# Rotary key at the front of the layer on 128 partitions, raw latents into their own norm, GLA values scaled by ScalarE

## Chip, cores, metric

The kernel runs on one core of one Trainium2 chip. The metric is the device time in microseconds (us) of one execution. Engines are called as in the profile: PE (TensorE matmuls), PEld (its weight loads), DVE (VectorE), ACT (ScalarE), POOL (GpSimd), SP (the queue that issues most DMAs). Matrix products run in a split form: each operand is written as a high part and a low part in a 32-bit matmul format, and three products (high·high, low·high, high·low) are added up.

## What is computed

Two layers of a hybrid encoder on 1024 tokens of width 1024. Cut to what the change touches:

```python
u = rmsnorm(h, ln_mix[i]) @ w_in[i]
(c_q, c_kv, k_rope, gate_a, gq, gk, gv, lr_f, lr_b, gate_g) = split_cols(u, IN_SPLITS)
# mla_branch
q  = (rmsnorm(c_q, q_norm) @ w_uq)          # q_nope and q_rope of 4 heads
kv = (rmsnorm(c_kv, kv_norm) @ w_ukv)       # k_nope and v of 4 heads
k_r = apply_rope(k_rope, pos)               # [x1*cos - x2*sin, x1*sin + x2*cos], one key for all heads
s = qn @ k_nope^T + qr @ k_r^T ; prob = softmax(s * scale) ; o = prob @ v
# gla_branch: gq, gk, gv with decays, in chunks, forward and backward, then a norm per head
h = h + concat(mla * silu(gate_a), gla * silu(gate_g)) @ w_out[i]
h = h + sigmoid(rmsnorm(h, ple_norm[i]) @ w_ple_gate[i]) * (p[i] @ w_ple_proj[i])
```

The first norm is never applied to x. The kernel multiplies the raw x (with the gain folded in) by w_in, and scales each product afterwards by r_x, the reciprocal root mean square of each token.

## The kernel before, in words

Everything is kept with features on partitions and the 1024 tokens along the free axis. SBUF tiles of 128x1024 come from one pool of 41 buffers (`mt`), PSUM from two tags, "mm" and "aux", with two buffers of 128x1024 each. A matmul tile of the input projection (`in_tile`) is 48 matmuls of 512 columns into one PSUM buffer; the buffer comes free when the last engine that reads it is done. Weights are loaded raw by SP (L141, two buffers), split by ACT into high part (L142) and negated copy (L146), and the low part is finished by an adding DMA on POOL's queue (L147); five pairs of split halves are kept ahead.

Within a layer the order of steps is a string of two-character words (`ORDER`, L50 and L51), one letter for the step and one digit for the head or tile. The framework's planner then orders the instructions of each engine by that priority and by its own modelled times, so neighbouring steps interleave, and each engine runs its queue strictly in that order. The letters that matter here:

- K, Q: the two pairs of GLA keys and queries. `in_qk` L330 to L334: two DVE products with r_x out of PSUM per tile.
- R: `rotary_tables`, first layer only. cos and sin for 1024 positions, computed on 128 partitions as 4 blocks of 256 positions by 32 frequencies, and written to DRAM (`cosd`, `sind`, L274).
- V: `in_v` L337 to L357, GLA values of two heads with tokens on partitions; L354 scales each of two PSUM buffers by `rc`, the column form of r_x, on DVE.
- S, O: GLA state and output of a head. S holds a chain of 28 small DVE steps (L456) and the masked copy L468; O ends in an own norm: ACT copies and squares PSUM (L102, L497), ACT and DVE split the squares (L128, L129), PE adds them over partitions (L181).
- C, D: two and three latent tiles. `latent_tile` L503 to L508: DVE multiplies PSUM by r_x (L506), ACT squares the result (`SquareSum`, L211 or L214), DVE adds the squares up (L215).
- N, M: `latent_norm` L510 to L518, norm of the C or D latents and their split.
- G, A: gates of GLA and MLA. L362 is a DVE product of PSUM with r_x, L363 the Silu on ACT.
- X: `q_pairs` L570, the two rotary query tiles, which stay in the two "aux" PSUM buffers, and cos and sin read back from DRAM (L576).
- E: `rotary_key` L579 to L595. Rows 64 to 127 of `small` (made by `in_small`, L315, ahead of all steps) are rotated: six DVE products of 32x1024 (L584 to L589), two ACT copies (L591, L592) and two DVE differences (L594) of 64x1024. The result `ks`, `kl` is first read by the attention scores (L667).
- H, T: query heads (L597) and `rotary_queries` (L603): per half two DVE products out of the "aux" buffers (L609, L610), a sum (L611), a split, and DMAs into `qs` (L619).
- k, v, s, b: keys, values, scores and outputs of the attention (L625, L633, L656, L693).

`rstd` (L170) makes a reciprocal root: matmul with ones, transposition, three Newton steps on 128x32 tiles, transposition back.

Of the kernel before, what the change touches and what calls it, by code (L numbers as in the profile page):

```python
# [10 lines left out]
F32 = mybir.dt.float32  # L11
F32R = mybir.dt.float32r
# [7 lines left out]
P = 128  # L20
# [26 lines left out]


WTAG = "aux"
ORDER = ("K0 R0 Q0 G0+ Z0 V0 K1 S0 Z1 V1 O0 S1 Q1 D0 Z2 G1 G2 P0 O1 S2 C0 Z3 D1 C1 N0 D2 O2 S3 G3 M0 A0 O3 X0 A1 E0 A2 A3+ H0 k0 T0 s0 v0 H2 k1+ s1 k2 b0 H1 k3 s2 y1 b1 H3+ s3 b2 v1 s4 y0 y3 b3 y2 s5 b4 w0 w1+ s6 w2 b5 w3+ s7 w4 b6 w5+ s8 w6 w7 b7",  # L50
         "Q0 K0 Z0 V0 S0 Z1 V1 S1 Q1 K1 Z2 G0 O0 S2 G1 Z3 G2+ C0 O1 D0 O2 S3 G3 C1 N0 D1 D2+ O3 M0 X0 A0 A1 E0 A2 k0 y2 H0 A3 T0 s0 v0 H3 k1+ s1 H1 b0 H2 s2 k2 b1 s3 y0 k3+ b2 v1 s4 y3 y1 b3 s5 b4 w0 w1+ s6 w2+ b5 w3 s7 w4 b6 w5+ s8 w6+ w7 b7")  # L51

ENG = dict(at="V", qi="V", qb="P", og="P", gate="P", sq="V", kT="A", put="A", o="A", ple="A", hadd="V")
TCKW = {"schedule_with_timeline_sim": True}
# [3 lines left out]
def hybrid_encoder(ctx: ExitStack, tc: tile.TileContext, xT, pT, pos, vecs, w_in, wq, wk, wv,  # L58
# [10 lines left out]
    def dram(shape, name):  # L69
        return tc.dram_tile(shape, F32, name=name)  # L70
# [43 lines left out]
    def flat(t):  # L114
        return t.rearrange("p a b -> p (a b)")
# [51 lines left out]
                    nc.tensor.matmul(ps[:, c, :], lhsT=a, rhs=b[:, c * HC:(c + 1) * HC],  # L167
                                     start=(i == 0 and j == 0), stop=(i == n - 1 and j == 2))

    def rstd(acc, width, n=S, tmp=st, res=mt, col=None):  # L170

        if isinstance(acc, tuple):
            mat, parts = ones_r.bitcast(F32), acc
        else:
            mat, parts = ones_r, (tmp(dt=F32R, name="sqh"), tmp(dt=F32R, name="sql"))
            split(parts[0][:, :n], parts[1][:, :n], acc)
        ps = flat(bank2("aux"))
        for c in range(0, n, HC):
            w = slice(c, min(c + HC, n))
            for i, part in enumerate(parts):  # L180
                nc.tensor.matmul(ps[:, w], lhsT=mat, rhs=part[:, w], start=(i == 0), stop=(i == len(parts) - 1))  # L181
        r = res(name="rstd")
        nb = n // 32
        nc.vector.transpose(r[:, :n], ps[:, :n])
        a = cp.tile([P, 32], F32, tag="nwa", name="nwa", bufs=2)[:, :nb]
        y = cp.tile([P, 32], F32, tag="nwy", name="nwy", bufs=2)[:, :nb]
        t = cp.tile([P, 32], F32, tag="nwt", name="nwt", bufs=2)[:, :nb]

        nc.vector.tensor_scalar(a, r[:, :n].rearrange("p (b i) -> p b i", i=32)[:, :, 0], 0.5 / width, 0.5 * EPS,
                                op0=ALU.mult, op1=ALU.add)  # L190
        nc.vector.tensor_scalar(y.bitcast(I32), a.bitcast(I32), 1, None, op0=ALU.arith_shift_right)
        nc.vector.tensor_scalar(y.bitcast(I32), y.bitcast(I32), -1.0, float(0x5F3759DF - 2 ** 22 - 2 ** 31),
                                op0=ALU.mult, op1=ALU.add)
        for _ in range(3):
            nc.vector.tensor_tensor(t, y, y, op=ALU.mult)
            nc.vector.tensor_tensor(t, t, a, op=ALU.mult)
            nc.vector.scalar_tensor_tensor(y, t, -1.5, y, op0=ALU.add, op1=ALU.mult)
        if col is not None:
            for g in range(4):
                nc.vector.tensor_copy(col[g * 32:(g + 1) * 32], y.rearrange("p (b g) -> p g b", g=4)[g * 32:(g + 1) * 32, g])  # L200
        nc.vector.transpose(r[:, :n], y.unsqueeze(2).to_broadcast((P, nb, 32)))
        return r
# [15 lines left out]
    h1d = dram([8, P, S], "h1d")  # L218
    cosd = dram([32, S], "cosd")
    sind = dram([32, S], "sind")  # L220

    def ple_projection(i):
        ops = []
# [12 lines left out]
        for g in range(4):  # L236
            hi, lo = load_split(w_proj[i, g], HC)
            for c in range(2):
# [4 lines left out]
                copy("ple", o, flat(ps))  # L243
                nc.sync.dma_start(projd[i][g * 2 + c], o)

    def rotary_tables():

        n = S // 4

        work = mt(name="rot")  # L250
        kk, ang, *rs = (work[:, i * n:(i + 1) * n] for i in range(4))
        posi = kk.bitcast(I32)
        for b in range(4):
            nc.sync.dma_start(posi[b * 32:(b + 1) * 32], pos[:, b * n:(b + 1) * n].to_broadcast((32, n)))
        nc.vector.tensor_copy(ang, posi)
        nc.vector.tensor_scalar(ang, ang, vec[:, V_INV:V_INV + 1], None, op0=ALU.mult)
        MAGIC = 12582912.0
        TWO_PI = 2.0 * np.pi
        C1 = 6.28125
        C2 = float(np.float32(np.round((TWO_PI - C1) * 2 ** 20) / 2 ** 20))  # L260
        C3 = float(np.float32(TWO_PI - C1 - C2))
        for r, dst, quarter in zip(rs, (sind, cosd), (0.0, 0.25)):
            nc.vector.tensor_scalar(kk, ang, 1.0 / TWO_PI, quarter, op0=ALU.mult, op1=ALU.add)
            nc.vector.tensor_scalar(kk, kk, MAGIC, None, op0=ALU.add)
            nc.vector.tensor_scalar(kk, kk, -MAGIC, None, op0=ALU.add)
            nc.vector.scalar_tensor_tensor(r, kk, -C1, ang, op0=ALU.mult, op1=ALU.add)
            nc.vector.scalar_tensor_tensor(r, kk, -C2, r, op0=ALU.mult, op1=ALU.add)
            nc.vector.scalar_tensor_tensor(r, kk, -C3, r, op0=ALU.mult, op1=ALU.add)
            if quarter:
                nc.vector.tensor_scalar(r, r, float(np.pi / 2), None, op0=ALU.add)  # L270
            nc.vector.tensor_scalar(r, r, 3.1415925, -3.1415925, op0=ALU.min, op1=ALU.max)
            nc.scalar.activation(r, r, AF.Sin)
            for b in range(4):
                nc.sync.dma_start(dst[:, b * n:(b + 1) * n], r[b * 32:(b + 1) * 32])  # L274
# [13 lines left out]
    for L in range(DEPTH):  # L288
# [7 lines left out]


        rc = cp.tile([P, 8], F32, tag="rc", name="rc", bufs=2)
        r_x = rstd(sq.acc, D, col=rc)

        afb = mt(name="afb").rearrange("p (d t c) -> p d t c", d=2, c=CH)
        nc.gpsimd.memset(afb, 0.0)
# [34 lines left out]
        def in_v(pair):  # L337

            ps = [flat(bank2(tag)).rearrange("p (t c) -> p t c", c=2 * P) for tag in ("mm", "aux")]
            for b in range(4):  # L340
                src = w_in[L, T_GV + 2 * pair + b // 2]
                hi, lo = load_split(src[:, (b % 2) * HC:(b % 2 + 1) * HC], HC)
                for k in (2 * b, 2 * b + 1):
                    c = slice((k % 2) * 2 * P, (k % 2 + 1) * 2 * P)
                    for t in range(8):
                        tok = slice(t * P, (t + 1) * P)
                        for n, (x_, w_) in enumerate(((xs[k][0], hi), (xs[k][0], lo), (xs[k][1], hi))):
                            nc.tensor.matmul(ps[t // 4][:, t % 4, :], lhsT=x_[:, tok], rhs=w_[:, c],
                                             start=(k == 0 and n == 0 and t % 2 == 0),
                                             stop=(k == 7 and n == 2 and t % 2 == 1))  # L350
            res = []
            for half in range(2):
                v = mt(name="gv").rearrange("p (t c) -> p t c", c=2 * P)
                nc.vector.tensor_tensor(v, ps[half], rc[:, half * 4:half * 4 + 4].unsqueeze(2).to_broadcast((P, 4, 2 * P)),  # L354
                                        op=ALU.mult)
                res.append(v)
            return [[res[t // 4][:, t % 4, h * P:(h + 1) * P] for t in range(8)] for h in range(2)]  # L357

# [143 lines left out]

        def latent_tile(t, s2, tile=mt):  # L503
            ps = in_tile(t)
            o = tile(name="craw")
            nc.vector.tensor_tensor(o, flat(ps), r_x, op=ALU.mult)  # L506
            s2.add(o)
            return o  # L508

        def latent_norm(raws, s2, off, width):  # L510
            r = rstd(s2.acc, width)
            res = []
            for j, raw in enumerate(raws):
                nc.vector.scalar_tensor_tensor(raw, raw, gv(off, j), r, op0=ALU.mult, op1=ALU.mult)
# [63 lines left out]

        def rotary_key():  # L579

            cos, sin = xx[2:]
            t1, t2 = mt(name="t1"), mt(name="t2")
            k1, k2 = slice(64, 96), slice(96, 128)
            nc.vector.tensor_tensor(t1[0:32], small[k1], cos[k1], op=ALU.mult)  # L584
            nc.vector.tensor_tensor(t2[0:32], small[k2], sin[k2], op=ALU.mult)
            nc.vector.tensor_tensor(t1[32:64], small[k1], sin[k1], op=ALU.mult)
            nc.vector.tensor_tensor(t2[32:64], small[k2], cos[k2], op=ALU.mult)
            nc.vector.tensor_tensor(t1[0:32], t1[0:32], t2[0:32], op=ALU.subtract)
            nc.vector.tensor_tensor(t1[32:64], t1[32:64], t2[32:64], op=ALU.add)  # L589
            ks, kl = mt(F32R, "ks"), mt(F32R, "kl")  # L590
            nc.scalar.activation(ks[0:64], t1[0:64], AF.Copy)  # L591
            nc.scalar.activation(ks[64:128], t1[0:64], AF.Copy)  # L592
            for half in (slice(0, 64), slice(64, 128)):
                nc.vector.tensor_tensor(kl[half], t1[0:64], ks[0:64].bitcast(F32), op=ALU.subtract)  # L594
            ksl.extend((ks, kl))  # L595

        def q_head(h):  # L597
# [344 lines left out]
```

## Time and profile before

| | |
|---|---|
| median of 3 runs | 1467.03 us (1465.24 to 1467.93) |
| the profiled execution, its own time | 1462.53 us |
| its span, first to last instruction | 1460.8 us |
| PE busy | 1379.5 us |
| DVE busy | 863.2 us |
| ACT busy | 720.7 us |
| mean granted clock of PE | 0.981 |

The page gives busy time by engine and the costliest groups of instructions. The trace answers further questions: who waited for whom, all instructions in order of time (idle time of the engine before an instruction stands in square brackets with what ended it), and busy times by stretch. Times within the execution count from the first instruction. Layer one runs its projection and GLA steps from about 57 to 383 us and its attention to about 630; layer two from about 757 to 1069 and to about 1300.

### The profile page before, as it was taken

Reading aid. Unit: us, or ns where it says so; the run is one execution under the profiler, and the core shown is the slowest. Engines: PE = TensorE matmul, PEld = TensorE weight load, DVE = VectorE, ACT = ScalarE, POOL = GpSimd, SP = SyncE. Lnnn points to the kernel's source line nnn. Section 1 sums busy time; section 2 is a strip of 40 time slices with the busy share of each in tenths; the row PEclk is TensorE's granted clock in tenths of the full one; section 3 lists DMA queues with packets and bytes.
Section 4 is the critical chain, followed back from the end, with each engine's and each line's share of the span. In section 5 each row is a group of like instructions: output and inputs, shape, how many; then the busy total and the mean of one; then the engine's idle time right before and its main releaser. Section 6 shows DMA issues by size and latency. Waiting matters only on the chain. (4 is left out here: it accounts for less than half of the span.)

```text
span 1460.8 us, 21130 instructions
## 1 busy us (share of the span) xinstructions
PE 1379.5 (94%) x8400; PEld 1168.7 (80%) x8400; DVE 863.2 (59%) x1260; ACT 720.7 (49%) x1013; POOL 427.7 (29%) x312
## 2 busy tenths in 40 slices
PE   7999999999889999999999999889989999999985
PEld 6799778878678788888889877778877888878984
DVE  2576745788446544464455676667744564456547
ACT  6565475545345443364445555534444453346541
POOL 3421211212346454112432111211244564311210
PEclk9999999999999999999999999999999999999997
DMA  7663546345531223256765343334651212335863
GB/s 275 184 131 73 108 106 178 82 100 132 151 61 54 65 73 88 71 108 151 200 163 124 79 88 79 88 74 94 176 144 41 66 51 73 101 80 101 218 135 123
DMA packets 77794, 163.94 MB, mean 112 GB/s; under 512 B 9536, under 2 KB 17088, under 8 KB 77696
## 3 DMA queue, kind: packets, MB, share of 16 engines
q1 hardware_dynamic: 51200, 116.19, 26.0%
q0 software_dynamic: 26496, 46.41, 19.1%
q8 instruction: 66, 1.08, 0.3%
q14 instruction: 32, 0.26, 0.1%
HBM read 128.74 MB, written 25.43 MB: 106 GB/s over the span
## 5 line engine op out<-in xcount | busy, mean ns | idle before, releaser
L146 ACT ACTIVATE wl<-wr 128x512 fp32r<-128x512 f32 (+2 forms) x176 | 107.3, 610 | 311.5 <-PE ps L167 279.3
L675 POOL TENSOR_SCALAR sc<-sc,sums 128x1024 f32<-128x1024 f32 x64 | 182.0, 2856 | 101.7 <-DVE sums L674 83.7
L147 POOL DMA_DIRECT2D wl<-in_w_in x84 | 72.6, 877 | 349.1 <-ACT wl L146 311.3
L142 ACT ACTIVATE wh<-wr 128x512 fp32r<-128x512 f32 (+2 forms) x184 | 110.7, 603 | 34.5 <-PE ps L647 13.2
L673 ACT ACTIVATE sc<-ps,top 128x1024 f32<-128x1024 f32 x64 | 71.4, 1116 | 83.2 <-DVE top L671 72.8
L129 DVE TENSOR_TENSOR el<-ps,eh 128x1024 fp32r<-128x1024 f32 x64 | 78.0, 1221 | 46.8 <-ACT eh L128 45.8
L670 DVE TENSOR_REDUCE top<-ps 128x1 f32<-128x1024 f32 x64 | 78.2, 1222 | 43.3 <-PE ps L667 43.3
L167 PE MATMUL ps<-xh,wh 128*128 128x512 f32 x288 | 92.3, 401 | 8.7 <-DVE gate L362 4.6
L456 DVE SCALAR_TENSOR_TENSOR s<-s,last 64x128 f32<-64x128 f32 x208 | 77.0, 370 | 36.8 <-ACT s L102 29.9
L167 PE MATMUL ps<-x0h,wh 128*128 128x512 f32 x288 | 91.6, 400 | 7.1 <-DVE t L609 4.1
L167 PE MATMUL ps<-x0h,wl 128*128 128x512 f32 x288 | 91.5, 398 | 0.3 <-DMA wl<-in_w_in 0.3
L167 PE MATMUL ps<-xh,wl 128*128 128x512 f32 x288 | 91.4, 396 | 0.0
L167 PE MATMUL ps<-x0l,wh 128*128 128x512 f32 x288 | 91.0, 397 | 0.0
L167 PE MATMUL ps<-xl,wh 128*128 128x512 f32 x288 | 90.8, 395 | 0.0
L167 PE MATMUL ps<-yh,wh 128*128 128x512 f32 x256 | 80.6, 392 | 0.9 <-DVE h L727 0.9
L128 ACT ACTIVATE eh<-ps 128x1024 fp32r<-128x1024 f32 x64 | 65.3, 1021 | 32.1 <-PE ps L688 30.6
L167 PE MATMUL ps<-yl,wh 128*128 128x512 f32 x256 | 79.5, 390 | 0.0
L167 PE MATMUL ps<-yh,wl 128*128 128x512 f32 x256 | 79.4, 391 | 0.0
L147 POOL DMA_DIRECT2D wl<-in_w_out x32 | 27.9, 872 | 169.5 <-ACT wl L146 168.8
L688 PE MATMUL ps<-ident,sc 128*128 128x128 f32 x512 | 66.5, 273 | 6.9 <-DVE ql L129 3.1
L688 PEld LDWEIGHTS ps<-ident,sc 128*128 128x128 f32 x512 | 59.2, 140 | 15.7 <-DVE ql L129 3.6
L167 PEld LDWEIGHTS ps<-xh,wh 128*128 128x128 f32 x288 | 54.4, 192 | 21.3 <-DVE gate L362 5.0
(258 smaller groups left out, 3576.8 us busy)
## 6 DMA issues: line engine op xcount, KB each, us to landing
wr<-in_w_in SPq DMA_DIRECT2D x88, 256.0 KB, 3.4
wl<-in_w_in POOLq DMA_DIRECT2D x84, 256.0 KB, 4.8
wr<-in_w_gate SPq DMA_DIRECT2D x40, 256.0 KB, 3.2
projd<-po SPq DMA_DIRECT2D x16, 512.0 KB, 4.1
wr<-in_w_out SPq DMA_DIRECT2D x32, 256.0 KB, 3.1
wl<-in_w_out POOLq DMA_DIRECT2D x32, 256.0 KB, 4.6
wl<-in_w_gate POOLq DMA_DIRECT2D x32, 256.0 KB, 4.7
xraw<-in_xT SPq DMA_DIRECT2D x8, 512.0 KB, 5.0
```

Of the source, the lines that this page charges most:

```text
L128: nc.scalar.activation(hi, src, AF.Copy)
L129: nc.vector.tensor_tensor(lo, src, hi.bitcast(F32), op=ALU.subtract)
L142: nc.scalar.activation(hi[:, :n], raw[:, :n], AF.Copy)
L146: nc.scalar.activation(lo[:, :n], raw[:, :n], AF.Copy, scale=-1.0)
L147: nc.gpsimd.dma_start(lo[:, :n], src, accum_op=ALU.add)
L167: nc.tensor.matmul(ps[:, c, :], lhsT=a, rhs=b[:, c * HC:(c + 1) * HC], start=(i == 0 and j == 0), stop=(i == n - 1 and j == 2))
L456: nc.vector.scalar_tensor_tensor(state(n)[rows], state(m)[rows], alpha[rows, m:m + 1], state(n)[rows], op0=ALU.mult, op1=ALU.add)
L670: nc.vector.tensor_reduce(m, flat(ps), axis=AX.X, op=ALU.max, negate=True)
L673: nc.scalar.activation(e, flat(ps), AF.Exp, bias=m, scale=SCALE, accum_out=sums[:, b:b + 1])
L675: nc.gpsimd.tensor_scalar(e, e, sums[:, b:b + 1], None, op0=ALU.mult)
L688: nc.tensor.transpose(out=ps[:, j, b * P:(b + 1) * P], in_=e[:, kt], identity=ident)
```

## The change

Three edits. The key's rotation moves from the end of the projection stage (after A1) to its front (E0 after R0 in layer one, after K0 in layer two), and works on 128 partitions: 8 DMAs bring the 64 rows of `small` into the 4-by-32 layout of the tables (which now stay in a constant tile `sc4`), six DVE products of 128x256 and one split of 128x512 follow, and 12 DMAs carry high and low part through DRAM (`krd`) into `ks` and `kl`, each stored twice. The latents leave PSUM by an ACT copy, without r_x, and their squares are taken by ACT straight from PSUM; the missing factor goes into the latents' norm through `base`, half the mean square plus half EPS of each token (kept in `ax`). The GLA values are scaled by eight ACT copies with a per-partition scale in place of two DVE products.

```diff
-... R0 Q0 G0+ ...            A1 E0 A2 A3+ H0 ...        (layer one)
+... R0 E0 Q0 G0+ ...         A1 A2 A3+ H0 ...
-Q0 K0 Z0 ...                 A1 E0 A2 k0 ...            (layer two)
+Q0 K0 E0 Z0 ...              A1 A2 k0 ...
     # rstd(..., ax=None, base=None)
+        if base is not None:
+            nc.vector.scalar_tensor_tensor(a, base, EPS, a, op0=ALU.mult, op1=ALU.add)
+        if ax is not None:
+            nc.vector.tensor_copy(ax, a)
     # in_v
-                nc.vector.tensor_tensor(v, ps[half], rc[...].unsqueeze(2).to_broadcast((P, 4, 2 * P)), op=ALU.mult)
+                for t in range(4):
+                    nc.scalar.activation(v[:, t], ps[half][:, t], AF.Copy, scale=rc[:, half * 4 + t:half * 4 + t + 1])
     # latent_tile
-            nc.vector.tensor_tensor(o, flat(ps), r_x, op=ALU.mult)
-            s2.add(o)
+            nc.scalar.activation(o, flat(ps), AF.Copy)
+            s2.add(flat(ps))
     # latent_norm
-            r = rstd(s2.acc, width)
+            r = rstd(s2.acc, width, base=ax)
     # rotary_key
-            (six products of 32x1024, two copies and two differences of 64x1024)
+            for b in range(4):
+                for k, row in ((k1, 64), (k2, 96)):
+                    nc.sync.dma_start(k[b * 32:(b + 1) * 32], small[row:row + 32, b * n:(b + 1) * n])
+            for x1, x2, o, op in ((cos, sin, rot[:, :n], ALU.subtract), (sin, cos, rot[:, n:], ALU.add)):
+                nc.vector.tensor_tensor(u1, k1, x1, op=ALU.mult)
+                nc.vector.tensor_tensor(u2, k2, x2, op=ALU.mult)
+                nc.vector.tensor_tensor(o, u1, u2, op=op)
+            split(parts[:, 0], parts[:, 1], rot)
+            for i, t in enumerate((ks, kl)):
+                for b in range(4):
+                    nc.sync.dma_start(krd[L, i, :, :, b * n:(b + 1) * n].rearrange("j f n -> f j n"),
+                                      parts[b * 32:(b + 1) * 32, i].bitcast(F32).rearrange("p (j n) -> p j n", j=2))
+                for half in (slice(0, 64), slice(64, 128)):
+                    nc.sync.dma_start(t[half].bitcast(F32), krd[L, i].rearrange("j f n -> (j f) n"))
```

## Rows read from the trace of the kernel before

**Rows 1.** The page's first part: span, and the busiest engine.

```profile
span 1460.8 us, 21130 instructions
PE 1379.5 (94%) x8400; PEld 1168.7 (80%) x8400; DVE 863.2 (59%) x1260; ACT 720.7 (49%) x1013; POOL 427.7 (29%) x312
```

**Rows 2.** PE's waits, whole run: line waited for, us in total, times, longest.

```profile
PE ps L167 <- DVE gate L362: 6.8, 2, 4.6
...
PE ps L181 <- ACT sqh L128: 5.9, 4, 3.7
...
PE ps L167 <- DVE t L609: 4.1, 1, 4.1
```

**Rows 3.** By stretch: busy PE, PEld, DVE, ACT, POOL; clock, DMA share.

```profile
100.00:120.00 20.00, 20.00 (x133) 17.92 (x133) 9.01 (x7) 6.99 (x13) 6.25 (x7) 1.00 0.57 119
...
360.00:380.00 20.00, 15.01 (x80) 13.09 (x81) 12.61 (x11) 5.06 (x9) 5.02 (x4) 0.91 0.52 117
```

**Rows 4.** DVE's groups from 340 to 360 us, one of the key's rotation.

```profile
L584 DVE TENSOR_TENSOR t<-small,cos 32x1024 f32<-32x1024 f32 x1 | 1.2, 1214 | 1.4 <-DMA cos<-cosd 1.4
```

**Rows 5.** DVE in order of time, 354 to 385: start, us, line, out<-in.

```profile
363.10 1.22 DVE L609 TENSOR_TENSOR t<-ps,cos 128x1024 f32<-128x1024 f32 x1
...
369.73 1.22 DVE L609 TENSOR_TENSOR t<-ps,sin 128x1024 f32<-128x1024 f32 x1
```

**Rows 6.** PE in order of time, 357 to 373: rows with idle time.

```profile
360.91 0.38 PE L647 MATMUL ps<-wh,ch 128*128 128x256 f32 x1 [1.53 <-DVE ql L129]
...
371.00 0.73 PE L167 MATMUL ps<-x0h,wh 128*128 128x512 f32 x2 [4.08 <-DVE t L609]
```

**Rows 7.** PE in order of time, 966 to 974 (layer two).

```profile
967.61 0.61 PE L167 MATMUL ps<-xl,wh 128*128 128x512 f32 x2
972.80 1.22 PE L167 MATMUL ps<-xh,wh 128*128 128x512 f32 x2 [4.58 <-DVE gate L362]
```

**Rows 8.** DVE in order of time, 955 to 980.

```profile
971.52 1.22 DVE L362 TENSOR_TENSOR gate<-ps,rstd 128x1024 f32<-128x1024 f32 x1
972.66 1.21 DVE L506 TENSOR_TENSOR craw<-ps,rstd 128x1024 f32<-128x1024 f32 x1
```

**Rows 9.** ACT in order of time, 955 to 980.

```profile
972.78 1.06 ACT L363 ACTIVATE gate<-gate 128x1024 f32<-128x1024 f32 x1 [4.45 <-DVE gate L362]
```

**Rows 10.** PE in order of time, 172 to 183 (layer one).

```profile
180.46 1.22 PE L167 MATMUL ps<-x0h,wh 128*128 128x512 f32 x2 [0.83 <-DVE gqk L333]
```

**Rows 11.** DVE in order of time, 1020 to 1076 (layer two).

```profile
1049.20 1.23 DVE L129 TENSOR_TENSOR kll<-ps,kh 128x1024 fp32r<-128x1024 f32 x1 [4.59 <-ACT kh L128]
```

**Rows 12.** ACT in order of time, 893 to 935 (layer two).

```profile
927.51 1.04 ACT L211 ACTIVATE acc<-craw 128x1024 f32<-128x1024 f32 x1
...
930.40 1.06 ACT L128 ACTIVATE sqh<-o 128x1024 fp32r<-128x1024 f32 x1
```

**Rows 13.** Groups by shape, whole run: xcount | busy us, mean ns of one.

```profile
L132 ACT ACTIVATE x0h<-xraw,vec 128x1024 fp32r<-128x1024 f32 x8 | 9.2, 1144 | 2.5 <-DMA xraw<-in_xT 2.5
...
L102 ACT ACTIVATE o<-ps 128x1024 f32<-128x1024 f32 x8 | 8.1, 1013 | 0.8 <-PE ps L488 0.8
...
L142 ACT ACTIVATE wh<-wr 128x256 fp32r<-128x256 f32 x8 | 3.3, 410 | 9.2 <-PE ps L647 9.1
...
L354 DVE TENSOR_TENSOR gv<-ps,rc 128x1024 f32<-128x1024 f32 x8 | 9.6, 1216 | 0.0
...
L841 DVE TENSOR_TENSOR gt<-gt,pj 128x288 f32<-128x288 f32 x8 | 3.6, 453 | 0.3 <-ACT gt L838 0.2
```

**Rows 14.** SP in order of time, 85 to 120 (layer one).

```profile
93.32 1.73 SPq L274 DMA_DIRECT2D cosd<-rot  x4
95.15 20.70 SPq L141 DMA_DIRECT2D wr<-in_w_in  x5
```

**Rows 15.** DMA issues, whole run: KB each, median us from issue to landing.

```profile
sind<-rot SPq DMA_DIRECT2D x4, 32.0 KB, 1.9
```

**Rows 16.** All engines in order of time, 222 to 226.

```profile
224.14 0.20 POOL L422 MEMSET s<- 64x128 f32 x1 [3.04 <-PE ps L181]
```

More of the change, by code (lines that the diff above doesn't have):

```diff
@@ L49 @@
 WTAG = "aux"
-ORDER = ("K0 R0 Q0 G0+ Z0 V0 K1 S0 Z1 V1 O0 S1 Q1 D0 Z2 G1 G2 P0 O1 S2 C0 Z3 D1 C1 N0 D2 O2 S3 G3 M0 A0 O3 X0 A1 E0 A2 A3+ H0 k0 T0 s0 v0 H2 k1+ s1 k2 b0 H1 k3 s2 y1 b1 H3+ s3 b2 v1 s4 y0 y3 b3 y2 s5 b4 w0 w1+ s6 w2 b5 w3+ s7 w4 b6 w5+ s8 w6 w7 b7",
-         "Q0 K0 Z0 V0 S0 Z1 V1 S1 Q1 K1 Z2 G0 O0 S2 G1 Z3 G2+ C0 O1 D0 O2 S3 G3 C1 N0 D1 D2+ O3 M0 X0 A0 A1 E0 A2 k0 y2 H0 A3 T0 s0 v0 H3 k1+ s1 H1 b0 H2 s2 k2 b1 s3 y0 k3+ b2 v1 s4 y3 y1 b3 s5 b4 w0 w1+ s6 w2+ b5 w3 s7 w4 b6 w5+ s8 w6+ w7 b7")
+ORDER = ("K0 R0 E0 Q0 G0+ Z0 V0 K1 S0 Z1 V1 O0 S1 Q1 D0 Z2 G1 G2 P0 O1 S2 C0 Z3 D1 C1 N0 D2 O2 S3 G3 M0 A0 O3 X0 A1 A2 A3+ H0 k0 T0 s0 v0 H2 k1+ s1 k2 b0 H1 k3 s2 y1 b1 H3+ s3 b2 v1 s4 y0 y3 b3 y2 s5 b4 w0 w1+ s6 w2 b5 w3+ s7 w4 b6 w5+ s8 w6 w7 b7",
+         "Q0 K0 E0 Z0 V0 S0 Z1 V1 S1 Q1 K1 Z2 G0 O0 S2 G1 Z3 G2+ C0 O1 D0 O2 S3 G3 C1 N0 D1 D2+ O3 M0 X0 A0 A1 A2 k0 y2 H0 A3 T0 s0 v0 H3 k1+ s1 H1 b0 H2 s2 k2 b1 s3 y0 k3+ b2 v1 s4 y3 y1 b3 s5 b4 w0 w1+ s6 w2+ b5 w3 s7 w4 b6 w5+ s8 w6+ w7 b7")
 ENG = dict(at="V", qi="V", qb="P", og="P", gate="P", sq="V", kT="A", put="A", o="A", ple="A", hadd="V")
@@ L168, in mm3, with rstd @@
                                      start=(i == 0 and j == 0), stop=(i == n - 1 and j == 2))
-    def rstd(acc, width, n=S, tmp=st, res=mt, col=None):
+    def rstd(acc, width, n=S, tmp=st, res=mt, col=None, ax=None, base=None):
         if isinstance(acc, tuple):
@@ L187, in rstd @@
         t = cp.tile([P, 32], F32, tag="nwt", name="nwt", bufs=2)[:, :nb]
-        nc.vector.tensor_scalar(a, r[:, :n].rearrange("p (b i) -> p b i", i=32)[:, :, 0], 0.5 / width, 0.5 * EPS,
-                                op0=ALU.mult, op1=ALU.add)
+        nc.vector.tensor_scalar(a, r[:, :n].rearrange("p (b i) -> p b i", i=32)[:, :, 0], 0.5 / width,
+                                0.0 if base is not None else 0.5 * EPS, op0=ALU.mult, op1=ALU.add)
+        if base is not None:
+            nc.vector.scalar_tensor_tensor(a, base, EPS, a, op0=ALU.mult, op1=ALU.add)
+        if ax is not None:
+            nc.vector.tensor_copy(ax, a)
         nc.vector.tensor_scalar(y.bitcast(I32), a.bitcast(I32), 1, None, op0=ALU.arith_shift_right)
@@ L220, in hybrid_encoder @@
     sind = dram([32, S], "sind")
+    krd = dram([DEPTH, 2, 2, 32, S], "krd")
     def ple_projection(i):
@@ L244, in ple_projection @@
                 nc.sync.dma_start(projd[i][g * 2 + c], o)
+    sc4 = cp.tile([P, 2, S // 4], F32, name="sc4")
     def rotary_tables():
@@ L250, in rotary_tables @@
         work = mt(name="rot")
-        kk, ang, *rs = (work[:, i * n:(i + 1) * n] for i in range(4))
+        kk, ang = (work[:, i * n:(i + 1) * n] for i in range(2))
+        rs = sc4[:, 1], sc4[:, 0]
         posi = kk.bitcast(I32)
@@ L298, in hybrid_encoder @@
         rc = cp.tile([P, 8], F32, tag="rc", name="rc", bufs=2)
-        r_x = rstd(sq.acc, D, col=rc)
+        ax = cp.tile([P, 32], F32, tag="ax", name="ax", bufs=2)
+        r_x = rstd(sq.acc, D, col=rc, ax=ax)
         afb = mt(name="afb").rearrange("p (d t c) -> p d t c", d=2, c=CH)
@@ L353, in in_v @@
                 v = mt(name="gv").rearrange("p (t c) -> p t c", c=2 * P)
-                nc.vector.tensor_tensor(v, ps[half], rc[:, half * 4:half * 4 + 4].unsqueeze(2).to_broadcast((P, 4, 2 * P)),
-                                        op=ALU.mult)
+                for t in range(4):
+                    nc.scalar.activation(v[:, t], ps[half][:, t], AF.Copy, scale=rc[:, half * 4 + t:half * 4 + t + 1])
                 res.append(v)
@@ L579, in rotary_key @@
         def rotary_key():
[L581 to L589, printed above, removed]
-            ks, kl = mt(F32R, "ks"), mt(F32R, "kl")
[L591 to L594, printed above, removed]
+            n = S // 4
+            work = mt(name="kr")
+            k1, k2, u1, u2 = (work[:, i * n:(i + 1) * n] for i in range(4))
+            rot = mt(name="krot")[:, :2 * n]
+            cos, sin = sc4[:, 0], sc4[:, 1]
+            for b in range(4):
[5 more added lines that the diff above has]
+                nc.vector.tensor_tensor(o, u1, u2, op=op)
+            parts = mt(F32R, "krp").rearrange("p (h c) -> p h c", h=2)
+            split(parts[:, 0], parts[:, 1], rot)
+            ks, kl = mt(F32R, "ks"), mt(F32R, "kl")
+            for i, t in enumerate((ks, kl)):
[4 more added lines that the diff above has]
+                    nc.sync.dma_start(t[half].bitcast(F32), krd[L, i].rearrange("j f n -> (j f) n"))
             ksl.extend((ks, kl))
```

## The prediction, made before the change was run

> **What bounds the kernel now.** I read the first part of the page, then PE's waits over the whole run, then the stretches in which they fall, in order of time. PE is busy for 1379.5 of 1460.8 us [rows 1], and nothing in the change removes a matmul. So the time can fall only where PE stands idle, and where its clock is granted low after such a stop. The other engines are far from full on the mean (DVE 59%, ACT 49%), and less busy time there is worth nothing by itself. In the projection and GLA steps PE's largest waits end with a DVE instruction that empties PSUM: 6.8 us in two waits for a gate's product, 4.1 us in one wait for a query product of T; one kind ends with ACT, 5.9 us for the high half of squares [rows 2]. The reader is to see that these are waits for a place in DVE's or ACT's queue, not for long instructions: each of those instructions takes 1.0 to 1.2 us. A stop of 4 us has a second price: the stretch 360 to 380 shows PE busy for only 15.0 us at a granted clock of 0.91 of full on the mean [rows 3]. The clock has two levels, 2.4 and 1.2 GHz, so 0.91 means about 3.6 us at the low one, and 20 x 0.09 = 1.8 us of work lost.
>
> **Edit one, the key's rotation.** Before, it is eight DVE instructions per layer on 32 or 64 partitions, each 1.21 us because the length is 1024 whatever the partitions [rows 4]: 8 x 1.21 = 9.7 us, and two ACT copies. In layer one they stand between 346 and 358 us, right ahead of T in DVE's queue. T's first half starts at 363.1 and its second at 369.7 [rows 5]; the third of its four products out of PSUM ends at 370.95, and PE, whose next gate tile needs one of the two "aux" buffers that T empties, starts at 371.00 after 4.08 us of idle time. Just before, PE waits 1.53 us for the split of a query head, which stands in the same queue [rows 6]. With 9.7 us less ahead of it T ends its third product at about 361.3. PE, without the 1.53 us, is through with the value matmuls that lie between only at about 365, so both waits go, and with them the low clock: 1.53 + 4.08 + 1.8 = **-7.4 us**. What is late next there is nothing within some 4 us; the scores that follow start 11 us later, behind the gate tile.
>
> In layer two the same 9.7 us go, but T gains nothing that I count: after the rotation DVE is idle for 4.59 us, waiting for ACT's copy of a key head [rows 11], so DVE has room there already. **0 us**.
>
> What is added at the front: six DVE products on 256 columns, for which the nearest row is 288 columns at 0.45 us, and the far one 1024 at 1.22 [rows 13]; I take 0.42, by length, so 2.5 us (at most 7.3). One split on 512 columns, about 0.6 us on ACT and 0.7 on DVE, lies between the 256 and 1024 column rows. It falls at about 95 to 110 us, where DVE is busy for 9.0 of 20 us and PE for all 20 [rows 3]: **0 us**, covered by DVE's idle 11 us; without that cover 3.2 us per layer. The result is needed some 280 us later.
>
> The 20 DMAs per layer go to SP's queue, in order with the raw weights. Eight loads cost 8 x 0.43 = 3.4 us of issue (four took 1.73) [rows 14]; then SP may stand until they have landed (1.9 us for the same 32 KB [rows 15]) and DVE and ACT are done (about 3.8); then eight stores at 3.4, a landing of 1.9, four loads at 1.7: 16 us in which weights queued behind them are not fetched, if the planner puts nothing in between. Against it: in the same stretch SP takes 20.7 us for five weight issues [rows 14], of which 5 x 0.43 is issuing and the rest, 18.5 us, is waiting for a free raw buffer, and five split pairs lie ahead of PE. So **0 us**; the bounds are 0 and 16 us per layer if the cover is gone. The Trainium skill's page "DMA: Bandwidth & Descriptors", section "Anatomy of one DMA", says that a DMA engine waits for no semaphore, the issuing queue does, and that most of a transfer's fixed cost is the receipt of the write. [...]
>
> The two results now occupy two of the 41 SBUF buffers from the front on, `small` gives one back. Counted by names, all 41 are taken at 224 us: 16 of x, 5 of r_x, masks and decay inputs, 2 latents, 2 of an output step, 2 gates, 4 of the embedding projection, 10 of GLA. Its sign in the trace is POOL clearing a state buffer at 224.14, when the matmuls on an earlier tile end [rows 16]. One buffer fewer shifts that state step by the few us until the next tile is freed. PE is given other work by the planner there, so I take **0 us**; without that it costs at most some 7, the length of a norm's small steps.
>
> **Edit two, the latents.** Ten DVE products of 1.21 us go [rows 8]; ten ACT copies of 1.01 us come, by the row of the same copy out of PSUM [rows 13]; squares are as many as before. Three 128x32 instructions per layer add about 0.6 us on DVE, off PE's path. Now a latent's PSUM buffer no longer waits behind the state chain on DVE. In layer two PE ends such a tile at 968.22, then stands for 4.58 us [rows 7]; the gate and the latent that hold the two "mm" buffers are emptied at 971.5 to 972.7 and 972.7 to 973.9, behind the state chain [rows 8]. ACT is idle there for 4.45 us [rows 9]. It would copy and square from 968.3 to 970.4, and PE would start at 970.4 in place of 972.8: **-2.4 us** (0 if the planner gives the tile the gate's buffer; -4.6 and 1.8 of clock if it puts other work in front). In layer one PE's start at 180.46, after 0.83 us for a GLA key's products [rows 10], could take the latent's buffer instead: **-0.8 us**. Against that, where ACT's queue is itself what PE waits for, a copy more is later: the squares' high half at 930.4 has a latent's square just before it at 927.5 [rows 12], and PE waits for it up to 3.7 us [rows 2]. **+1.0 us**; the bounds are 0 and 10 (all ten).
>
> **Edit three, GLA values.** Eight DVE products of 1.22 us become 32 ACT copies of 256 columns with a scale per partition. The trace has 256 columns at 0.41 us without such a scale, and a scale costs at most 1.144 - 1.013 = 0.13 [rows 13], so 0.41 to 0.54, and I take 0.49: 2.0 us per PSUM buffer in place of 1.22, 15.7 us of ACT in all. The first evacuation lies where ACT is busy for 7 of 20 us, DVE for 9 and PE for all 20 [rows 3]: **0 us** both ways; the bounds are 0 and 8 x 0.8 = 6 us. The Trainium skill's page "ScalarE: Activation LUTs" gives 186 ns plus 0.833 ns per element, 93 more for a scale from memory, and 93 of overlap back to back (section "What ACT_TABLE_LOAD costs"): 0.40 us each by that estimate, 12.8 us in all, and the same zero on PE's path.
>
> **The sum.** -7.4 - 2.4 - 0.8 + 1.0 = -9.6 us. The profiled execution's own time is 1462.5 us, with a span of 1460.8; it becomes 1452.9. The median of the runs is 1467.0, 4.5 above that execution, and I carry the difference over: **1457.4 us**.
>
> **The rivals.** All are given against the median.
>
> First, the gain is given back: the planner orders every queue anew, and a stop that goes at 371 returns elsewhere, as the one at 972 (4.58 us) arises from nothing but the order of a gate behind a state chain. One new stop of that size with its clock is 4.6 + 1.8 = 6.4, so 1457.4 + 6.4 = 1463.8 us. For it: waits of 3.7 to 4.6 us stand in three different places of the projection and GLA steps [rows 2]. Against it: DVE has 41 - 8 = 33 us less to do over both layers (34 instructions of 1.2 us go; twelve products, two differences and the small ones come).
>
> Second, slower: **ACT takes DVE's place**. Evacuations and splits of squares then wait in ACT's queue. The extra time is 10 x 1.0 + 15.7 = 26 us; all of it on PE's path gives 1457.4 + 25 = 1482 us, two thirds about 1474. It decides from the point where half, 13 us, ends up in PE's waits. For it: PE already waits 5.9 us for squares on ACT. Against it: ACT is idle at the very places where DVE is late. The Trainium skill's page on ScalarE, section "Rules for kernel authors", says that plain multiplications belong on VectorE, which speaks for this rival; the rows show 1.01 us on ACT against 1.21 on DVE for a whole evacuation, and only in pieces of 256 is ACT dearer.
>
> Third, slower: **the front starves**. SP is held for the 16 us in one piece, and raw weights come late. The spare of 18.5 us is used up if the rotation comes 3 us later than I think; one layer's full 16 gives 1457.4 + 16 = 1473 us. That the change does not do what it says (rotation still ahead of T) is excluded by its inputs, which are ready 270 us before.
>
> **How the numbers follow.** This kernel's measurement tells about 0.2%, 2.9 us, from no change. Chances: forecast 0.52, all faster; first rival 0.26 (0.11 faster, 0.13 within, 0.02 slower); second 0.14 (0.11 slower, 0.03 within); third 0.08 (0.06 slower, 0.02 within). So faster 0.63, within 0.18, slower 0.19. The range reaches down by the larger outcome at 972 (-4.0) and by more DVE-ended stops that shrink, some 7 us, to 1446, and up past the first rival into the lower half of the second, 1470.
>
> **What would show it.** Right: no idle time of PE above 1 us between the query projection and the first scores of layer one; the gate tile there not waiting for L609's successor; a latent tile followed by an ACT copy within 1 us of its last matmul; no wait for weights between 95 and 125 us and 765 and 800. Wrong: PE waits on ACT (copies of values or latents) in place of DVE; PE waits for a weight DMA at a layer's front; new waits behind the state chain; or the stop at 371 still there, held by something else than the key's rotation.

## The result, and the profile after

| | before | changed |
|---|---|---|
| median | 1466.5 us (4 runs) | 1486.5 us (4 runs, 1485.3 to 1487.3) |
| ratio to before, 95% interval | | 1.0139 [1.0121, 1.0157] |
| profiled execution, own time | 1462.5 us | 1487.3 us |
| its span | 1460.8 us | 1485.6 us |

The change is slower by 20.0 us, above the top of the forecast range (1470). The two profiled executions differ by 24.8 us, because the one of before lies 4.0 us below its median and the one of after 0.8 above. Line numbers below are those of each kernel itself; the changed file is longer, so L362 of before is L373, and so on.

First part of the page of after, to be held against [rows 1]:

```profile
span 1485.6 us, 21217 instructions
PE 1385.0 (93%) x8400; PEld 1173.4 (79%) x8400; DVE 828.0 (56%) x1246; ACT 735.5 (50%) x1051; POOL 427.1 (29%) x312
```

DVE lost 35 us of work, as planned, and PE needs 5.5 us more for the same 8400 matmuls. PE's waits of after (line waited for, us in total, times, longest), to be held against [rows 2]:

```profile
PE ps L182 <- ACT sqh L128: 11.4, 3, 5.5
PE ps L167 <- ACT gv L366: 7.9, 2, 5.9
...
PE ps L167 <- DVE gate L373: 4.9, 2, 4.6
PE ps L359 <- DVE afb L479: 4.6, 2, 3.3
PE ps L493 <- DVE afb L479: 4.3, 1, 4.3
PE ps L167 <- DVE t L629: 4.1, 1, 4.1
```

PE waits twice as long for squares, the wait for values on ACT is new, the waits for the masked copies of the GLA state (afb) have grown (4.6 and 4.3 us, where before has 2.4 and 1.4), and the 4.1 us for T's product are still there. PE in order of time, rows with idle time, layer one first (it answers [rows 6]), then layer two:

```profile
364.86 1.23 PE L167 MATMUL ps<-x0h,wh 128*128 128x512 f32 x2 [4.08 <-DVE t L629]
...
829.22 0.38 PE L359 MATMUL ps<-wh,xh 128*128 128x256 f32 x1 [3.34 <-DVE afb L479]
848.38 1.22 PE L167 MATMUL ps<-xh,wh 128*128 128x512 f32 x2 [5.91 <-ACT gv L366]
...
996.87 1.22 PE L167 MATMUL ps<-xh,wh 128*128 128x512 f32 x2 [4.58 <-DVE gate L373]
```

Layer one is 5.3 us faster up to its last step (the output product that waits 0.86 us for DVE's sum h starts at 616.12 in place of 621.40); 2.5 us of that lie before PE's first norm matmul (54.87 in place of 57.38), where no step of the change has begun. The whole loss lies in layer two's projection and GLA steps. From the matmul of the first decay Z0 to the first score product with the rotated key (ks), by stretch (length, busy PE, PEld, DVE, ACT, POOL, then clock and DMA share), first before, then after:

```profile
776.00:1069.40 293.40, 277.14 (x2184) 235.48 (x2183) 203.51 (x317) 150.89 (x219) 58.89 (x59) 0.98 0.44 102
```

```profile
770.70:1093.60 322.90, 285.74 (x2184) 242.40 (x2182) 182.86 (x309) 159.68 (x239) 58.14 (x59) 0.94 0.43 99
```

The same 2184 matmuls take 29.5 us more: 20.9 of that is idle time (37.2 in place of 16.3 us), and 8.6 is PE being busy longer at a mean granted clock of 0.94 in place of 0.98, that is with more of its time at 1.2 GHz. So a stop's second price, 41% of the first here, was close to the 1.8 us for 4.08 of the prediction (44%), but it was paid and not saved.

### The profile page after: what moved, and what is told of

Same layout as the page of the kernel before. It is cut to its first block, busy times and chain, and to the rows that moved or that the text cites. A ratio compares the mean times of both kernels' runs of the same rounds, so it can differ in the third digit from the quotient of the medians.

```text
span 1485.6 us, 21217 instructions
## 1 busy us (share of the span) xinstructions
PE 1385.0 (93%) x8400; PEld 1173.4 (79%) x8400; DVE 828.0 (56%) x1246; ACT 735.5 (50%) x1051; POOL 427.1 (29%) x312
## 5 line engine op out<-in xcount | busy, mean ns | idle before, releaser
L708 PEld LDWEIGHTS ps<-ident,sc 128*128 128x128 f32 x512 | 59.2, 140 | 15.7 <-DVE ql L129 3.6
```

Of the source, the lines that this page charges most:

```text
L708: nc.tensor.transpose(out=ps[:, j, b * P:(b + 1) * P], in_=e[:, kt], identity=ident)
```

## Experiments

**One edit at a time.** My first theory on seeing the values' waits was rival two, ACT taking DVE's place. Three kernels have one edit each; a fourth has edits one and two.

The key alone:

> Edit one alone: the key's rotation at the front, latents and values left on DVE. Values theory (ACT as the engine that empties the GLA values costs layer two its 30 us): this kernel has none of it, keeps layer one's 5.3 us, and comes to about 1461 us. Key theory (the early rotation, its DMAs, its two held buffers or the order that the planner makes of them cost layer two the time): about 1486. Reorder theory (no single edit, the order that falls out of the three together): anywhere from 1455 to 1480, and the three single edits do not add up to the +20 of the whole. In each, the 4.1 us wait for T's product in layer one stays if it is T's own, and goes if the rotation ahead of it caused it.

The latents alone:

> Edit two alone: latents leave PSUM by ACT, squares from PSUM. Values theory: within 4 us of the kernel before, about 1467. Latents theory (ACT's copies stand ahead of the squares that PE waits for): 1475 or more, with PE's waits for the high half of squares up from 5.9 us to 10 or more. Key theory: 1467. My prediction's steps for this edit gave -2.2, so about 1464, with the 4.58 us stop for the gate in layer two cut to 2.2.

The values alone:

> Edit three alone: GLA values by 32 ACT copies. Values theory: layer two loses most of its 30 us, so about 1485 to 1495, with stops of PE of 2 to 6 us that end with ACT's copies of values, and clock lost behind them. Latents and key theories: about 1467. Prediction's step: 1467 (0 us), at most 1473.

All but the values:

```diff
-                for t in range(4):
-                    nc.scalar.activation(v[:, t], ps[half][:, t], AF.Copy, scale=rc[...])
+                nc.vector.tensor_tensor(v, ps[half], rc[...].unsqueeze(2).to_broadcast((P, 4, 2 * P)), op=ALU.mult)
```

> The changed kernel with the values back on DVE (edits one and two). Values theory: about 1461, the loss in layer two gone. Latents or key theory: about 1480 to 1486. Reorder theory: any value, not the sum of the two single kernels' differences.

Measured, as ratio to before: key alone 1483.3 us, 1.0103 [1.0076, 1.0129]; latents alone 1466.0, 0.9997 [0.9980, 1.0013]; values alone 1464.9, 0.9990 [0.9975, 1.0004]; key and latents 1485.9, 1.0120 [1.0092, 1.0149]. The key alone makes most of the loss (15 us by its ratio, 11 to 19; the whole change 20, 18 to 23), the other two edits alone none. The values theory falls, and rival two with it. The waits for values on ACT are a symptom: with the values on DVE, PE stands for them at the same place. Here are PE's rows with idle time from the kernel with the key alone:

```profile
830.16 0.58 PE L358 MATMUL ps<-wh,xh 128*128 128x256 f32 x1 [4.43 <-DVE afb L478]
848.21 0.70 PE L167 MATMUL ps<-xh,wh 128*128 128x512 f32 x2 [3.83 <-DVE gv L364]
```

**Where the key's rotation holds layer two up.** ACT in order of time at the front of layer two, after. Z0's matmul on PE (L385) starts at 770.74; its bias and activation on ACT (tile z, L389) could follow at once. PE's row first, then ACT's:

```profile
770.74 0.63 PE L385 MATMUL ps<-lr,wzt 96*128 96x512 f32 x2
```

```profile
770.79 0.62 ACT L142 ACTIVATE wh<-wr 128x512 fp32r<-128x512 f32 x1
778.48 0.63 ACT L146 ACTIVATE wl<-wr 128x512 fp32r<-128x512 f32 x1 [7.07 <-DMA kr<-small]
779.01 0.62 ACT L142 ACTIVATE wh<-wr 128x512 fp32r<-128x512 f32 x1
783.02 0.63 ACT L128 ACTIVATE krp<-krot 128x512 fp32r<-128x512 f32 x1 [3.39 <-DVE krot L605]
...
788.32 0.63 ACT L146 ACTIVATE wl<-wr 128x512 fp32r<-128x512 f32 x1 [3.62 <-PE ps L359]
...
789.37 1.10 ACT L389 ACTIVATE z<-ps,vec 128x1024 f32<-128x1024 f32 x1
```

ACT stands idle three times, and z starts 18.6 us after its matmul. Before, it is 0.67 us:

```profile
776.02 0.63 PE L374 MATMUL ps<-lr,wzt 96*128 96x512 f32 x2
```

```profile
776.69 1.12 ACT L378 ACTIVATE z<-ps,vec 128x1024 f32<-128x1024 f32 x1
```

Two theories: ACT's queue (the key's split waits for loads and products, z behind it), or the order in which SBUF buffers are given out: z and a are named (asked for in the program's order of steps) behind the rotation's kr, krot, krp, ks and kl, and the planner places no tile of the pool before those named ahead of it have their first use, however many buffers are free. (Counted by names in the trace of the key alone, 25 to 28 of the 41 are in use from 786 to 806 us.) The first kernel takes the split off ACT; the second only touches all five tiles at the rotation's start, that is, writes one column of each; the third names them one step later.

```diff
-            split(parts[:, 0], parts[:, 1], rot)
+            nc.vector.tensor_copy(parts[:, 0], rot)
+            nc.vector.tensor_tensor(parts[:, 1], rot, parts[:, 0].bitcast(F32), op=ALU.subtract)
```

> Edit one alone, with the split of the rotated key taken off ACT: its high part is made by a DVE copy, so ACT has no instruction of the rotation at all. ACT-queue theory (the key's split, which waits for eight loads and six products, stands ahead of the decay chain in ACT's queue): z is at about 775, and the time about 1461. Buffer-order theory: z still comes 15 us late, behind three weight splits, and the time stays at about 1483 (1479 to 1487).

```diff
-            work = mt(name="kr")
...
+            work, rot_, parts, ks, kl = mt(name="kr"), mt(name="krot"), mt(F32R, "krp"), mt(F32R, "ks"), mt(F32R, "kl")
+            for o in (work, rot_, parts, ks, kl):
+                nc.gpsimd.memset(o[:, S - 1:S].bitcast(F32), 0.0)
```

> Edit one alone, the rotation at the same place in the order, with the same work. The only difference from the run with the key alone (1483 us): all five SBUF tiles of the rotation are asked for at its start and touched by a one-column write on POOL, so that none of them is first used late. Buffer-order theory (the pool hands its buffers out in the order in which the program names them, so the decay's z and a, named behind the rotation's ks and kl, cannot be placed until ks and kl are, though a dozen buffers are free): z follows its matmul within 2 us at about 775 instead of 18 us later, and the time comes to about 1461, 1456 to 1466. Queue theory (ACT, DVE or SP is held by the rotation's own instructions): stays at 1480 to 1486. Two-buffers theory (41 buffers less two): stays at 1480 to 1486.

```diff
-         "Q0 K0 E0 Z0 V0 S0 ...
+         "Q0 K0 Z0 E0 V0 S0 ...
```

> Edit one alone, with the rotation one word later in layer two (Z0 E0 in place of E0 Z0): its tiles are named behind those of the first decay. Buffer-order theory: layer two's loss goes, about 1461 us (1456 to 1468); its tiles now stand ahead of the GLA values' alone. Two-buffers theory (two of the 41 buffers are held by the key from the front on): unchanged, about 1483. SP theory (20 more DMAs ahead of the weights): unchanged, 1475 to 1485.

Split on DVE: 1485.2 us, 1.0126 [1.0110, 1.0143]; all touched: 1461.4, 0.9969 [0.9948, 0.9989]; one step later: 1464.8, 1.0000 [0.9985, 1.0014]. ACT in order of time, first with the split on DVE (Z0's matmul at 772.02), then with all five touched (773.65):

```profile
790.65 1.10 ACT L388 ACTIVATE z<-ps,vec 128x1024 f32<-128x1024 f32 x1
```

```profile
774.32 1.12 ACT L388 ACTIVATE z<-ps,vec 128x1024 f32<-128x1024 f32 x1
...
792.08 0.62 ACT L128 ACTIVATE krp<-krot 128x512 fp32r<-128x512 f32 x1
```

With no instruction of the rotation on ACT, z is as late as ever. With the same work at the same place in the order of steps and five one-column writes more, z is on time and the loss is gone; the rotation's own split then stands 17.8 us behind z, where it stands 6.4 us ahead of z with the key alone. The kernel one step later also excludes the two held buffers and the 20 DMAs as causes of the 20 us: it has both.

**Which tiles.** Was it the late tiles, or the writes on POOL as such?

```diff
-            for o in (work, rot_, parts, ks, kl):
+            for o in (work, rot_, parts):
```

> Edit one alone; all five tiles are asked for at the rotation's start, but only the three that are used early anyway (work, krot, krp) are touched by POOL. ks and kl are first written by the last DMAs, as in the changed kernel. Buffer-order theory (the first use of each tile in the program's order, the last being kl): nothing gained, z at about 791 us, 1480 to 1487. Touch theory (the writes on POOL change the planner's queues by themselves, whatever tile they touch): about 1461.

```diff
-            for o in (work, rot_, parts, ks, kl):
+            for o in (ks, kl):
```

> The same with only ks and kl touched; krot and krp are first used by DVE's third product and by ACT's split, at about 783 and 785 us. Buffer-order theory: z stands right behind the key's split on ACT, at 786 to 787 us, between 774 (all touched) and 791 (none), and the time lies between 1461 and 1484, about 1470 to 1478. Touch theory: 1461, as with all five; if only ks and kl mattered: 1461, z at 774.

Three early tiles touched: 1482.0 us, 1.0120 [1.0104, 1.0137]. ks and kl touched: 1482.9, 1.0126 [1.0110, 1.0141]. In the first, ACT's z stands beside SP's first use of ks, without needing it (kl follows at 792.76; the planner goes by its own modelled times, so the trace shows the order to about a microsecond):

```profile
791.28 1.10 ACT L388 ACTIVATE z<-ps,vec 128x1024 f32<-128x1024 f32 x1
```

```profile
791.39 1.13 SPq L614 DMA_DIRECT2D ks<-krd  x2
```

In the second, z is right behind the first use of krp, the last tile left untouched:

```profile
786.25 0.63 ACT L128 ACTIVATE krp<-krot 128x512 fp32r<-128x512 f32 x1 [3.23 <-DVE krot L607]
786.79 1.10 ACT L388 ACTIVATE z<-ps,vec 128x1024 f32<-128x1024 f32 x1
```

So the place of z is the one that buffer order gives in every placement, and the touch theory falls. The time of the second kernel was missed: I expected a middle loss for a middle delay, and the whole loss came. All kernels fall in two groups:

| kernel | z after its matmul, us | median, us | ratio |
|---|---|---|---|
| before | 0.7 | 1464.0 to 1466.5 | 1 |
| latents alone; values alone | 0.7 | 1466.0; 1464.9 | 0.9997; 0.9990 |
| key, all touched | 0.7 | 1461.4 | 0.9969 |
| key one step later | 0.7 | 1464.8 | 1.0000 |
| all three edits, all touched | 0.7 | 1460.4 | 0.9968 |
| key, ks and kl touched | 12.7 | 1482.9 | 1.0126 |
| key, three touched; on DVE; alone | 18.6 | 1482.0; 1485.2; 1483.3 | 1.0120; 1.0126; 1.0103 |
| key and latents; changed kernel | 18.6 | 1485.9; 1486.5 | 1.0120; 1.0139 |
| T's products moved ahead, four kernels (below) | 0.7 | 1460.1 to 1466.8 | 0.9955 to 1.0016 |

In the kernels with a late z the head's state matmuls come only after half of the next values (PE's L440 at 815.44 after, its equal L429 at 803.83 before), and PE runs a query tile between the two halves. That this is the point from which the delay costs all is argued from the order; no kernel places z between 0.7 and 12.7 us.

**T's stop in layer one.** The 4.08 us for T's product stayed to the hundredth. DVE in order of time with the key alone:

```profile
353.86 1.23 DVE L129 TENSOR_TENSOR ql<-ps,qh 128x1024 fp32r<-128x1024 f32 x1 [4.04 <-ACT qh L128]
356.77 1.22 DVE L129 TENSOR_TENSOR kll<-ps,kh 128x1024 fp32r<-128x1024 f32 x1 [1.69 <-ACT kh L128]
357.92 1.22 DVE L628 TENSOR_TENSOR t<-ps,cos 128x1024 f32<-128x1024 f32 x1
```

DVE idles 5.7 us for the splits of H0 and k0, which wait for ACT's copies (at 352.82 and 355.74) and those for PE's own matmuls, and T stands behind them. T at 357.9 is 5.2 us earlier than in [rows 5], but PE reaches its gate tile 5.7 us earlier as well (361.2 in place of 366.9), and the stop is what it was. Three kernels put T ahead of H0 and k0 in layer one (with the key after Z0, with the key touched, and with the key at its old place):

```diff
-... A2 A3+ H0 k0 T0 s0 ...
+... A2 A3+ T0 H0 k0 s0 ...
```

> The kernel with the rotation after Z0, and in layer one the query products T0 ahead of H0 and k0 in the order. The stop of 4.08 us for T's third product stayed in every kernel with the early key. T theory (T stands behind the splits of a query head and of a key head, which wait 4 and 1.7 us for ACT and PE, while DVE is idle): the stop goes, and 4 to 6 us against the kernel with the rotation after Z0, so about 1456. Rival (the aux buffers are only one of the limits: the next is the stop for scores or for the gate behind it): within 2 us of it.

> Edit one alone with the touch and T0 ahead of H0 and k0 in layer one. T theory: about 1458, 2 to 5 us under the same without T's move (1461.4), the same as with all three edits within 3 us. Rival: 1461.

> The kernel before, its key's rotation at its old place, with only T0 put ahead of H0 and k0 in layer one. My prediction put the stops of 1.53 and 4.08 us in layer one down to the eight key products ahead of T in DVE's queue. If that were so, the stop for T's product stays here (the eight products are still ahead of T), 1465 to 1467. If the stop is T's own place behind the splits of H0 and k0, it goes here as well, and the time is 1 to 5 us lower, 1461 to 1465, perhaps with a new stop for a key head's split.

Measured: 1460.1 us, 0.9955 [0.9938, 0.9972], against 1464.8 without T's move; 1461.2, 0.9966 [0.9954, 0.9977], against 1461.4; and for the key at its old place 1466.8, 1.0016 [1.0003, 1.0029]. PE's rows with idle time, first with the key after Z0, then with the key at its old place:

```profile
372.54 1.22 PE L686 MATMUL ps<-kh,qh 128*128 128x512 f32 x2 [4.23 <-ACT kh L128]
```

```profile
364.78 1.22 PE L167 MATMUL ps<-x0h,wh 128*128 128x512 f32 x2 [6.66 <-DVE t L609]
380.70 0.36 PE L647 MATMUL ps<-wh,ch 128*128 128x256 f32 x1 [2.88 <-DVE ql L129]
```

T has at least two holders, one behind the other: the eight key products (with them ahead, T's stop stays and grows to 6.66) and the splits of H0 and k0 (without them and without the key products, T's stop goes, and a stop of 4.23 us for k0's split takes its place). Whether T's move gives anything is not settled. By the medians of the four pairs (the fourth is below) it gives 4.7 us with the key after Z0, of which only 1.6 show from PE's first norm matmul to the output product at the end of layer one (561.2 and 559.7 us), and 0.2 with the key touched; it costs 2.0 with the key at its old place, and 4.1 with all three edits.

**All three edits, mended.**

> All three edits, with the rotation's five tiles touched at its start (the only difference from the changed kernel, 1486 us). Buffer-order theory: the whole loss goes, 1457 to 1463 us; edits two and three add nothing that can be measured to the key alone with the same touch (1461.4). Rival (values and latents on ACT cost several us of their own, hidden so far behind the larger loss): 1466 or more, with PE's waits for values on ACT (7.9 us in the changed kernel) still there.

> The same, with T0 ahead of H0 and k0 in layer one. T theory: 2 to 5 us less than all three edits with the touch, about 1457, no stop for T's product and a stop of some 4 us for a key head's split in its place, as in the run with T first. Rival: no difference.

All three with the five tiles touched: 1460.4 us, 0.9968 [0.9957, 0.9978], that is 4.7 us under before by this ratio and 26 under the change as made, with no wait for values among PE's waits. T ahead as well: 1464.5, 1.0000 [0.9988, 1.0013], where about 1457 was expected. T's stop is back there at 359.57 with 4.12 us, and the one for k0's split at 376.60 comes on top. Neither of the two holders stands ahead of T there, but its first product waits for cos, 3.11 us against 1.43 with the key touched and T ahead, where T's stop is gone:

```profile
347.13 1.22 DVE L630 TENSOR_TENSOR t<-ps,cos 128x1024 f32<-128x1024 f32 x1 [3.11 <-DMA cos<-cosd]
```

That this wait is the third holder is not shown. The best versions here lie between 0.9955 and 0.9969 and are not told apart: the key after Z0 with T ahead, the key alone with the touch (with T ahead or not), and all three edits with the touch.

## Why the prediction was wrong, step by step

**What bounds the kernel, and what a stop costs.** Right. PE's idle time and the clock behind it make up the whole 29.5 us, 20.9 and 8.6.

**Edit one, layer one, -7.4.** About half came, and most of that by luck. From PE's first norm matmul to the end of T's stop the changed kernel takes 310.0 us (54.87 to 364.86), before 313.6 (57.38 to 371.00): 3.6 less; the key alone 4.1, the key touched 2.3. Of the sum's terms only the 1.53 us came; the rest of the gain arose at places that the prediction does not name (the last section has one). The failed step is "right ahead of T in DVE's queue", and with it "What is late next there is nothing within some 4 us": DVE's splits for H0 and k0 stand between the key's products and T. DVE in order of time, before:

```profile
359.67 1.18 DVE L129 TENSOR_TENSOR ql<-ps,qh 128x1024 fp32r<-128x1024 f32 x1
...
361.96 1.22 DVE L129 TENSOR_TENSOR kll<-ps,kh 128x1024 fp32r<-128x1024 f32 x1
```

Their wait had been hidden by the very products that were removed, so T came earlier by no more than PE did, and the 4.08 us stayed.

**Edit one, layer two, 0.** The sum of its work was right: with the tiles touched, the stretch from Z0's matmul to the scores takes 294.0 us against 293.4. The failed step is the SBUF pool, put at 0 us and "at most some 7". I counted how many buffers the key holds, and at the front of layer two the pool had a dozen free. (In layer one, where I had counted all 41 as taken, POOL's clearing of a state buffer did move, from 224.14 to 227.33 us, and PE has no new wait there.) What cost the 15 to 20 us was the order: tiles that are named early and first used late stop those named behind them.

**What edit one adds at the front.** Sizes were right, covers held. From the changed kernel, by line (min/median/max in ns):

```profile
L603 DVE TENSOR_TENSOR kr<-kr,sc x4: 425/426/427, 85.0 to 781.8; 128x256 f32<-128x256 f32 x4
L601 SPq DMA_DIRECT2D kr<-small x16: 507/592/1489, 71.6 to 777.6; - x16
...
DMA to landing us min/median/max: 1.8/4.0/6.2
```

Products took 0.43 us (0.42 forecast), the split 0.63 on ACT and 0.69 on DVE. The way through SP was longer than my 16 us: with the key alone, 25.3 us from the first load's issue (769.05) to the last one of kl (794.35). SP in order of time:

```profile
769.05 1.28 SPq L600 DMA_DIRECT2D kr<-small  x2
...
775.93 5.34 SPq L600 DMA_DIRECT2D kr<-small  x6
...
793.27 1.08 SPq L613 DMA_DIRECT2D kl<-krd  x2
```

The eight loads alone are issued over 12.2 us in place of 3.4, as the planner puts a raw weight and two copies of GLA keys between them and six of them take 5.34 us; they land after 4.0 us on the median and not after 1.9. (These are times from issue to landing; no run here shows what they are made up of.) PE did not starve because of it: with the key alone and the five tiles touched the same way takes 36.3 us (769.78 to 806.08) and there is no loss, and PE's one wait for a weight of layer two's projection, 1.3 us in the changed kernel at 818.83, is small. Rival three fell.

**Edit two, -2.2.** Nothing that can be measured came (-0.4 us, -2.9 to +1.9). The stop at 972 stayed. ACT in order of time from the kernel with the latents alone, and PE's row:

```profile
976.90 1.06 ACT L369 ACTIVATE gate<-gate 128x1024 f32<-128x1024 f32 x1 [4.46 <-DVE gate L368]
977.86 1.01 ACT L513 ACTIVATE craw<-ps 128x1024 f32<-128x1024 f32 x1
```

```profile
976.92 1.22 PE L167 MATMUL ps<-xh,wh 128*128 128x512 f32 x2 [4.59 <-DVE gate L368]
```

The failed step is that ACT, idle there for 4.45 us, "would copy and square" at once: ACT is not free, it waits with the gate's Silu at the head of its queue, and the latent's copy stands behind that, as the product did on DVE. The -0.8 in layer one did not come either: PE's wait for a GLA key there is 1.75 us (at 180.64) in place of 0.83. The +1.0 for the squares is not shown: that wait is 4.58 in place of 3.75 us at the same place, but over the run the waits for squares add up to 5.8 us (5.9 before), and with the key touched, which has no copies of latents on ACT, the same wait is 5.43.

**Edit three, 0.** Right: 0.9990 [0.9975, 1.0004]. The copies are L366 of the changed kernel:

```profile
L366 ACT ACTIVATE gv<-ps,rc x16: 454/480/510, 805.9 to 849.3; 128x256 f32<-128x256 f32 x16
```

They took 0.48 us each in layer two, where 0.49 was taken from the rows. Back to back they overlap, which the 15.7 us for all 32 left out; ACT in order of time:

```profile
807.16 1.94 ACT L366 ACTIVATE gv<-ps,rc 128x256 f32<-128x256 f32 x5
```

Five take 1.94 us, 0.39 each. From figures of the Trainium skill's page "ScalarE: Activation LUTs" (section "What ACT_TABLE_LOAD costs"), which count such an overlap, the prediction had the estimate of 0.40, and the trace agrees. The page's rule that multiplications belong on VectorE ("Rules for kernel authors") speaks of cost per element; here the time did not depend on it, as PE did not wait for these copies unless the decay was late.

**The rivals.** The sign was on the side of the two slower ones, but neither was the cause. The first came nearest in kind, a queue ordered anew, and was priced at one stop of 6.4 us where there were many (20.9 us of idle time), it seems because the delay of one decay passes on through the states and outputs that follow. What would have shown it beforehand is a list of the tiles that the moved step names, with when each is first used, and of the steps named behind it. The listed signs pointed the right way, except that "PE waits on ACT" was read there as a sign of ACT's load.

## To carry to other kernels

When a step moves ahead of others in a planned order, ask of each SBUF tile that it names when it is first used: a tile first used late holds back every tile named behind it, with a dozen buffers free. Name such tiles after the steps on the critical path, or touch them at once. And when work ahead of a wait is removed, take the next item's own inputs into account: if it waits for the very engine that is to be freed, the stop moves along with it.

## What the runs showed of the chip

A stop of the same length need not cost the same. Before and with the key alone PE stands 2.2 us for the same gate (at 316.43 and 314.03), and after it, in the stretch 316 to 330 us, the granted clock was, first before, then with the key alone:

```profile
316.00:330.00 14.00, 13.57 (x83) 10.96 (x85) 13.18 (x31) 5.19 (x6) 1.12 (x2) 0.88 0.31 84
```

```profile
316.00:330.00 14.00, 14.00 (x177) 11.71 (x176) 13.31 (x27) 4.55 (x6) 1.73 (x2) 1.00 0.40 92
```

That is 1.7 us, as much as the stop itself nearly, in one and none in the other; with the 1.53 us it makes up the key alone's gain from there to the end of T's stop (54.6 us before, 51.2 with the key alone). What PE did between is also different there (83 matmuls against 177), so the cause is open. And the stretch up to PE's first norm matmul, in which these kernels have the same work, took 54.6 to 58.0 us in the executions shown, so differences of a few us from the start of the span say nothing of the change.
